# A DeepNorm layer with MoBA attention and 32 experts: routing chain in another order, V in the half slot of x transposed, two activation tiles and one Y buffer in a half slot

## The chip, the cores and the metric

The kernel runs on one core of a Trainium2 chip. Five engines work side by side, each through its own queue in program order: TensorE (PE in the rows; its weight loads are PEld), VectorE (DVE), ScalarE (ACT), GpSimd (POOL) and SyncE (SP), whose queue issues the DMA transfers. The metric is the device time of one launch in microseconds, and the number reported is the median of the runs.

## What is computed

One layer over 256 tokens of width 1024, in fp32. With the configuration cut to what is used:

```python
# attention: 8 heads of 128; 256 tokens are one block, so it is plain causal attention
# with a relative position bias
h = layer_norm(ALPHA * x + attention(x) @ w_out)
# mixture of experts: 32 experts, each token goes to its 4 best
logits = h @ w_router + b_router
top_logit, top_e = lax.top_k(logits, 4);  gate = softmax(top_logit)
# per expert, over the tokens that chose it
g, u = split(h @ w_gu[e] + b_gu[e])          # 1024 -> 2 x 1024
g = minimum(g, 7);  u = clip(u, -7, 7)
act = g * sigmoid(1.702 * g) * (u + 1)       # the swiglu
y = act @ w_down[e] + b_down[e]
out = layer_norm(ALPHA * h + sum over the 4 of gate * y)
```

The expert weights are 32 x 12 MB; together with the attention weights some 424 MB are read once.

## The kernel before, in words

**Weights.** `W_SLOTS` = 13 slots of 2 MB in SBUF, [128, 4096] fp32 each, hold everything large. `todo` lists all weight pieces in the order of use: six of `w_in`, two of `w_out`, then for every expert four of gate/up ("gu") and two of down ("dn"). Each time a slot comes free (`drop`, `done`) `prefetch` issues the next transfers on SP's queue (line 139), as many as there are free slots. The instruction that issues a load into a used slot waits until the matmuls that read the old contents have run; that wait stands in SP's queue, in order. Some slots hold no weights: `xhl` (the split of x), `BT_xT` (two halves: BT, later x and h; xT, later the accumulator `acc`), `QT_KTt` (two halves: QT, later the experts' biases; KTt, later the transposed rows `rT` and then `first`), `V`, and from the first expert on `acts_Ys`. That one holds three activation tiles g7, sg, u7, the transposed activation `aT`, and two buffers `Ys` for the outputs of a pair of experts.

**Order.** The program is scheduled by hand: every engine runs its instructions in the order in which the code issues them. There are eight PSUM banks with fixed names: `o0`, `o1`, `tp0`, `tp1`, `tp2`, `hg`, `hu`, `yp`. `o_tile()` hands out o0 and o1 in turn, `tp_tile()` tp0, tp1, tp2. A matmul into a bank waits until its last reader is done.

**Routing chain.** After the last piece of the attention's output projection (`out_part(3, ...)`, L431 to L434), for each of two token halves t: `residual` on VectorE (L440, with a piece of the statistics at L441, L191), the mean and the root (`Stats.root`, `finish`), the transposes of the rows (`rows_T`, L449) with a copy by ScalarE, the logits (L492, 16 matmul records of 32 columns), the four best (`top_experts`, VectorE, L499 to L504), the positions of the tokens in their experts' lists (`positions`, a matmul with a triangular matrix, L510), read by VectorE (`read_positions`, L514), one-hot matrices (L520), and the gather of the first pair's rows as matmuls with them (`first_gather`, L531). The two gather banks are zeroed ahead of that by an fp32 matmul of 512 columns each whose operands give zero (`open_gather`, L525). `stage1_bias` (L549) opens the banks hg and hu with the expert's bias, over 32 rows. Then stage 1 of expert 0 begins (L644).

**Experts.** Two experts make a pair, with 64 places for tokens each. For every expert the code issues, in this order: stage 1 (`stage1`, gate/up, L644, 64 matmul records per bank pair and weight piece); the `swiglu` on VectorE and ScalarE (L651, L652 on ScalarE, L653, L654, L655); half of the scatter of the pair before it (`pair_scatter`, L700, one token half t = s: a matmul into o0 and one into o1, each read by an add of VectorE into `acc`, L695); in odd experts from 3 on the gather of the next pair in two halves, the first ahead of the activation's transposes and the second behind them (L630; ScalarE reads the first half at L543, VectorE the second at L541); the transposes of the activation (`act_T`, L661) with a copy by ScalarE (L662); and stage 2 (`stage2`, down, L672). A matmul of fp32 with 512 columns is two records in the trace. Experts 17 and 19 also take in the residual (`add_residual`, each one half of the columns; L721 and L722 are its two steps on VectorE per token half, with a scratch value `tmp` in `first`), and expert 21 makes the list of experts with more than 64 tokens (`overflow_list`). Behind the last expert `more_blocks` loops over that list, and the last layer norm follows.

The lines that set the order around the change:

```python
            act = swiglu(hgu)
            Y = Ys[:, p % 2]
            if GT is not None:
                pair_scatter(GT, Y_old, s, p == 1)
```

## Time and profile before

| what | value |
|---|---|
| median of 3 runs | 1064.25 us (1064.24 to 1067.23) |
| the profiled execution | 1066.63 us |
| its span in the trace | 1064.8 us |
| TensorE matmul busy | 1017.2 us (96% of the span), 5008 records |
| VectorE busy | 261.5 us (25%) |
| ScalarE busy | 177.1 us (17%) |
| GpSimd busy | 7.4 us (1%) |
| moved by DMA | 425.33 MB, mean 399 GB/s; 426 to 429 GB/s in nearly every fortieth of the span from 160 us to 1010 us |

The profile's times are microseconds from the start of the span. A share of busy time is an average over stages with different limits, so the views by stretch and the waits are read beside it. "<-" in a row stands between an instruction's output and its inputs; in brackets behind a row is how long its engine had been idle before it, and whose end let it start.

### The profile page before, as it was taken

What the parts mean: (1) busy time and instruction counts of PE and PEld (TensorE: products, weight loads), DVE (VectorE), ACT (ScalarE), POOL (GpSimd) and SP (SyncE); (2) the same over time, 40 slices, a digit from 0 to 9 for tenths busy, and PEclk for the clock granted to TensorE, in tenths of its full rate; (3) what the DMA queues carried; (4) which work ended last, traced back from release to release, by engine and by line L of the source; (5) the groups of instructions that cost most, each with busy time, mean ns of one, the idle gap of its engine ahead of it and who ended that gap; (6) DMA issues with size and microseconds to landing.
All of it is one profiled execution on the core that took longest, in us unless ns stands there. A gap on an engine that the chain in (4) does not pass through costs nothing. (4 is left out here: it accounts for less than half of the span.)

```text
span 1064.8 us, 11698 instructions
## 1 busy us (share of the span) xinstructions
PE 1017.2 (96%) x5008; PEld 453.3 (43%) x5008; DVE 261.5 (25%) x554; ACT 177.1 (17%) x343; POOL 7.4 (1%) x8
## 2 busy tenths in 40 slices
PE   9999999999999999999999999999999999999994
PEld 8988743343433334343434343343434343434431
DVE  5576421121121111121212141211212121212114
ACT  5455121010100101010101010010101010101112
POOL 0000100000000000000000000000000000000001
PEclk9999799999999999999999999999999999999996
DMA  8987769999999999999999999999999999999971
GB/s 302 421 367 260 305 267 429 428 428 427 428 427 428 428 426 428 426 429 427 427 429 427 428 428 427 428 427 428 427 428 428 426 428 427 428 429 426 427 334 41
DMA packets 33110, 425.33 MB, mean 399 GB/s; under 512 B 3640, under 2 KB 4960, under 8 KB 7424
## 3 DMA queue, kind: packets, MB, share of 16 engines
q1 hardware_dynamic: 32784, 423.51, 94.4%
q10 hardware_dynamic: 272, 1.05, 0.3%
q8 instruction: 41, 0.67, 0.3%
q14 instruction: 13, 0.11, 0.0%
HBM read 423.48 MB, written 1.06 MB: 399 GB/s over the span
## 5 line engine op out<-in xcount | busy, mean ns | idle before, releaser
L644 PE MATMUL hg<-w,xg 128*64 128x512 f32 x960 | 248.2, 595 | 0.0
L644 PE MATMUL hu<-w,xg 128*64 128x512 f32 x960 | 246.6, 592 | 0.0
L672 PE MATMUL yp<-w,acts_Ys 128*64 128x512 f32 x1008 | 228.1, 598 | 11.2 <-ACT acts_Ys L662 11.2
L651 DVE TENSOR_SCALAR acts_Ys<-hg 128x512 f32<-128x512 f32 x32 | 22.1, 692 | 662.1 <-PE hg L644 653.6
L672 PEld LDWEIGHTS yp<-w,acts_Ys 128*64 128x64 f32 x1008 | 70.9, 137 | 146.1 <-issue 128.9
L644 PEld LDWEIGHTS hg<-w,xg 128*64 128x64 f32 x960 | 66.2, 137 | 144.3 <-issue 144.3
L644 PEld LDWEIGHTS hu<-w,xg 128*64 128x64 f32 x960 | 68.9, 137 | 137.2 <-issue 137.2
L652 ACT ACTIVATE acts_Ys<-acts_Ys 128x512 f32<-128x512 f32 x32 | 20.1, 630 | 459.5 <-DVE acts_Ys L651 459.5
L676 ACT COPY acts_Ys<-yp 64x512 f32<-64x512 f32 x63 | 36.5, 580 | 244.0 <-PE yp L672 236.9
L630 PE MATMUL tp<-OH,BT_xT 128*128 128x128 f32 x480 | 60.1, 279 | 9.7 <-ACT xg L543 9.7
L630 PEld LDWEIGHTS tp<-OH,BT_xT 128*128 128x128 f32 x480 | 56.7, 192 | 20.6 <-ACT xg L543 13.0
L700 PE MATMUL o<-acts_Ys,QT_KTt 128*128 128x512 f32 x120 | 59.5, 618 | 0.0
L166 DVE TENSOR_TENSOR whl<-w,whl 128x1024 fp32r<-128x1024 f32 (+1 forms) x36 | 38.2, 1103 | 23.5 <-ACT whl L177 23.5
L695 DVE TENSOR_TENSOR BT_xT<-o,BT_xT 128x512 f32<-128x512 f32 x60 | 38.6, 682 | 0.4
L700 PEld LDWEIGHTS o<-acts_Ys,QT_KTt 128*128 128x128 f32 x120 | 20.3, 189 | 38.7 <-issue 26.5
L177 ACT CAST whl<-w 128x1024 fp32r<-128x1024 f32 (+1 forms) x36 | 32.7, 955 | 15.3 <-DMA w<-in_w_in 6.3
L549 PE MATMUL hg<-QT_KTt,c 32*64 32x512 f32 x128 | 34.8, 620 | 0.0
L541 DVE TENSOR_SCALAR xg<-tp,c 128x128 f32<-128x128 f32 x60 | 20.5, 403 | 55.0 <-PE tp L630 55.0
L549 PE MATMUL hu<-QT_KTt,c 32*64 32x512 f32 x128 | 32.7, 587 | 0.0
L543 ACT ACTIVATE xg<-tp,c 128x128 f32<-128x128 f32 x60 | 22.6, 456 | 49.3 <-PE tp L630 49.3
L661 PE MATMUL tp<-c,acts_Ys 128*128 128x128 f32 x128 | 19.7, 277 | 6.7 <-DVE acts_Ys L655 6.7
L662 ACT COPY acts_Ys<-tp 128x512 f32<-128x512 f32 x32 | 18.9, 590 | 40.1 <-PE tp L661 40.1
(245 smaller groups left out, 723.1 us busy)
## 6 DMA issues: line engine op xcount, KB each, us to landing
w<-in_w_gu SPq DMA_DIRECT2D x128, 2048.0 KB, 28.7
w<-in_w_dn SPq DMA_DIRECT2D x63, 2048.0 KB, 27.5
w<-in_w_in SPq DMA_DIRECT2D x3, 2048.0 KB, 16.2
w<-in_w_in SPq DMA_DIRECT2D x4, 1024.0 KB, 11.1
w<-in_w_out SPq DMA_DIRECT2D x2, 2048.0 KB, 25.4
w<-in_w_dn SPq DMA_DIRECT2D x4, 512.0 KB, 30.0
w<-in_w_in SPq DMA_DIRECT2D x4, 256.0 KB, 5.0
w<-in_w_in SPq DMA_DIRECT2D x2, 512.0 KB, 7.9
```

The lines of the kernel that those rows point to most:

```text
L166: nc.vector.tensor_tensor(lo[:, s], w[:, s], hi[:, s].bitcast(F32), op=OP.subtract)
L177: nc.scalar.copy(o, i)
L541: nc.vector.tensor_scalar(o, i, g, b, op0=OP.mult, op1=OP.add)
L543: nc.scalar.activation(o, i, AF.Identity, scale=g, bias=b)
L549: nc.tensor.matmul(hgu[i][s * 64:(s + 1) * 64], onehot_e, bgu[:, 2 * i + s, :], start=True, stop=False)
L630: nc.tensor.matmul(ps[:, k * 128:(k + 1) * 128], h[:, t, kk * 128:(kk + 1) * 128], OH[:, t].rearrange("p s c -> p (s c)"), start=t == 0, s ...
L644: nc.tensor.matmul(hgu[i][s * 64:(s + 1) * 64], xg(k), w[:, kk, q * 512:(q + 1) * 512], start=False, stop=k == KT - 1)
L651: nc.vector.tensor_scalar(g7, hgu[0], LIMIT, None, op0=OP.min)
L672: nc.tensor.matmul(y_ps[s], aT[:, kk % 4, kk // 4, :], w[:, k, HALVES[s ^ swap]], start=kk == 0, stop=kk == KT - 1)
L676: copy(Y[s * 64:(s + 1) * 64, s ^ swap, :], y_ps[s])
L695: nc.vector.tensor_tensor(d, po, d, op=OP.add)
L700: nc.tensor.matmul(po, GT[:, cb, t, :], Y[:, cb, :], start=True, stop=True)
```

## The change

1. **V.** `V`, `first` and the biases take other halves: V lies where x transposed and later `acc` lie, `first` (the one-hots and gathered rows of the first pair) there too. The slot `V` is gone, with the `drop()` that gave it back.
2. **Activations.** Two activation tiles g7 and sg instead of three, with `aT` in g7's place, and one `Y` buffer instead of two, all in the half KTt. The clipped up half is written back to its PSUM bank (hu). The slot `acts_Ys` and the reserve that kept it free are gone. GT, the transposed gates, has a tile of its own, and `more_blocks` a slot `spare`.
3. **Scatter.** Both token halves of the pair's scatter follow stage 1 of the even expert, since Y is written again at its end; the odd expert has none.
4. **Residual.** `tmp` in `add_residual` lies in the banks o0 and o1.
5. **Routing chain.** The residuals are split from the statistics (`count`); logits of the first half are interleaved; the second half's experts are picked ahead of reading the first half's positions; the first expert's bias moves up to right behind the first positions; the gather banks are zeroed by bf16 matmuls with a tile of zeros; `filler(2)` puts two such matmuls ahead of the second half's gather; `rows_T` opens a bank per piece, with o0 for the third.
6. **Constants.** The constant tile shrinks from 641 to 452 columns, and `overflow_list` uses `ones`.

The core of the diff:

```diff
-    (BT, xT), (QT, KTt), (V, _) = (halves(slot(n)) for n in ("BT_xT", "QT_KTt", "V"))
-    x, acc, V = (t.rearrange("p (t d) -> p t d", t=2) for t in (BT, xT, V))
-    biases, first = QT, KTt
+    (BT, xT), (QT, KTt) = (halves(slot(n)) for n in ("BT_xT", "QT_KTt"))
+    x, acc = (t.rearrange("p (t d) -> p t d", t=2) for t in (BT, xT))
+    V, first, biases = acc, xT, QT
...
+    g7, sg = KTt[:, :512], KTt[:, 512:1024]
+    aT = g7.rearrange("p (j s c) -> p j s c", j=4, s=2)
+    Y = KTt[:, 1024:].rearrange("p (b c) -> p b c", b=2)
...
+    zeros = hp.tile([128, 512], BF, name="zeros")
...
         for ps in first_ps:
-            nc.tensor.matmul(ps, tri[:32, 0:1].to_broadcast([32, 128]), c[:32, :512], start=True, stop=False)
+            nc.tensor.matmul(ps, zeros[:, :128], zeros, start=True, stop=False)
+
+    def filler(n):
+
+        ps = bank("o0")
+        for i in range(n):
+            nc.tensor.matmul(ps, zeros[:, :128], zeros, start=i == 0, stop=i == n - 1)
...
+    logits(0, range(6, KT))
+    rows_T(1, 2, act_copy)
+    for i in range(3):
+        count(1, i)
+    logits(1)
     stats[1].root()
...
-    logits(1, range(6))
+    top_experts(0)
     stats[1].finish()
-    top_experts(0)
-    logits(1, range(6, KT))
     pp = positions(0)
+    hgu = stage1_bias(ident[:NE, 0:1].to_broadcast([NE, CAP]))
+    top_experts(1)
     read_positions(0, pp)
-    top_experts(1)
...
     pair_onehots(0, OH, slice(1, 2))
-    hgu = stage1_bias(ident[:NE, 0:1].to_broadcast([NE, CAP]))
+    filler(2)
     first_gather(1)
...
-        g7, sg, u7 = act3
+        u7 = hgu[1]
...
-        nc.vector.tensor_scalar(u7, hgu[1], LIMIT, -LIMIT, op0=OP.min, op1=OP.max)
+        nc.vector.tensor_scalar(u7, u7, LIMIT, -LIMIT, op0=OP.min, op1=OP.max)
...
-        tmp = first[:, :512]
         ps = tp_tile()
         spread(ps, 0, i)
         for t in range(2):
+            tmp = o_tile()
             nc.vector.scalar_tensor_tensor(tmp, h[:, t, cs], ALPHA, ps, op0=OP.mult, op1=OP.mult)
...
             act = swiglu(hgu)
-            Y = Ys[:, p % 2]
-            if GT is not None:
-                pair_scatter(GT, Y_old, s, p == 1)
+            if GT is not None and not s:
+                for t in range(2):
+                    pair_scatter(GT, Y, t, p == 1)
```

What it moves on the engines is shown at three places. A name ending in a number is one tile or one opening of a bank, "waits" names the engines whose semaphore the instruction waits for, and xN counts equal instructions in a row (two matmul records of the trace are one fp32 matmul here).

TensorE, the routing chain from the end of the logits to stage 1 of expert 0. tp0 and tp1 are the gather banks, M the chosen experts, hg and hu the banks of stage 1. Before:

```order
L492 MATMUL o1_1087<-oh_wg_83,QT_KTt_80 128x32 x8
L510 MATMUL tp2_1195<-M_954,c_68 128x32
L525 MATMUL tp0_1208<-c_68 128x512
L525 MATMUL tp1_1209<-c_68 128x512
L510 MATMUL tp2_1212<-M_954,ones_73 128x32
L510 MATMUL tp2_1212<-M_954,c_68 128x32
L531 MATMUL tp0_1208<-QT_KTt_80,BT_xT_79 128x128 x4
L531 MATMUL tp1_1209<-QT_KTt_80,BT_xT_79 128x128 x4
L549 MATMUL hg_1225<-QT_KTt_80,c_68 64x512 x2
L549 MATMUL hu_1226<-QT_KTt_80,c_68 64x512 x2
L531 MATMUL tp0_1208<-QT_KTt_80,BT_xT_79 128x128 x4
L531 MATMUL tp1_1209<-QT_KTt_80,BT_xT_79 128x128 x4
```

The same stretch of TensorE's queue now, from right behind the first half's positions (L508) to the filler; the second half's gather follows:

```order
L553 MATMUL hg_1199<-QT_KTt_80,c_68 64x512 x2
L553 MATMUL hu_1200<-QT_KTt_80,c_68 64x512 x2
L523 LDWEIGHTS zeros_84
L523 MATMUL tp0_1216<-zeros_84 128x512
L523 LDWEIGHTS zeros_84
L523 MATMUL tp1_1217<-zeros_84 128x512
L508 MATMUL tp2_1220<-M_955,ones_73 128x32
L508 MATMUL tp2_1220<-M_955,c_68 128x32
L535 MATMUL tp0_1216<-BT_xT_79 128x128 x4
L535 MATMUL tp1_1217<-BT_xT_79 128x128 x4
L529 LDWEIGHTS zeros_84
L529 MATMUL o0_1233<-zeros_84 128x512
```

The bias (hg, hu) has moved from between the two gathers to behind the first positions, the zeroing reads the tile of zeros, and zero matmuls into o0 stand ahead of the second half's gather.

TensorE, even expert 26, from the end of stage 1 (L644, now L651) to stage 2 (L672, now L679). o0 and o1 take the scatter, tp2 the activation's transposes. Before:

```order
L644 MATMUL hu_4069<-w_3938,xg_4001 64x512 x2
L700 MATMUL o0_4119<-acts_Ys_1311,QT_KTt_80 128x512 [waits Activation_49]
L700 MATMUL o1_4122<-acts_Ys_1311,QT_KTt_80 128x512
L661 MATMUL tp2_4125<-c_68,acts_Ys_1311 128x128 [waits DVE_49,PE_49]
L661 MATMUL tp2_4125<-c_68,acts_Ys_1311 128x128 x3
L672 MATMUL yp_4131<-w_3956,acts_Ys_1311 64x512 [waits DMAHW3_49,Activation_49]
```

The same stretch now:

```order
L651 MATMUL hu_4090<-w_3954,xg_4021 64x512 x2
L707 MATMUL o0_4140<-QT_KTt_80,GT_4046 128x512 [waits Activation_49]
L707 MATMUL o1_4143<-QT_KTt_80,GT_4046 128x512
L707 MATMUL o0_4146<-QT_KTt_80,GT_4046 128x512 [waits DVE_49]
L707 MATMUL o1_4149<-QT_KTt_80,GT_4046 128x512 [waits DVE_49]
L668 MATMUL tp2_4152<-c_68,QT_KTt_80 128x128 [waits PE_49]
L668 MATMUL tp2_4152<-c_68,QT_KTt_80 128x128 x3
L679 MATMUL yp_4158<-w_3964,QT_KTt_80 64x512 [waits DMAHW3_49,Activation_49]
```

Two scatter matmuls have become four, and the third and fourth wait for VectorE.

VectorE, the same expert, before:

```order
L651 TENSOR_SCALAR acts_Ys_1311<-hg_4068 128x512 [waits DVE_49,PE_49]
L653 TENSOR_SCALAR acts_Ys_1311<-hu_4069 128x512 [waits PE_49]
L654 TENSOR_TENSOR acts_Ys_1311<-acts_Ys_1311 128x512 [waits Activation_49]
L655 SCALAR_TENSOR_TENSOR acts_Ys_1311<-acts_Ys_1311 128x512 [waits DVE_49]
L695 TENSOR_TENSOR BT_xT_79<-o0_4119,BT_xT_79 128x512 [waits PE_49]
L695 TENSOR_TENSOR BT_xT_79<-o1_4122,BT_xT_79 128x512 [waits PE_49]
```

And now:

```order
L658 TENSOR_SCALAR QT_KTt_80<-hg_4089 128x512 [waits PE_49,Activation_49]
L660 TENSOR_SCALAR hu_4090<-hu_4090 128x512 [waits PE_49]
L661 TENSOR_TENSOR QT_KTt_80<-QT_KTt_80 128x512 [waits Activation_49]
L662 SCALAR_TENSOR_TENSOR QT_KTt_80<-hu_4090,QT_KTt_80 128x512 [waits DVE_49]
L702 TENSOR_TENSOR BT_xT_79<-o0_4140,BT_xT_79 128x512 [waits PE_49]
L702 TENSOR_TENSOR BT_xT_79<-o1_4143,BT_xT_79 128x512 [waits PE_49]
L702 TENSOR_TENSOR BT_xT_79<-o0_4146,BT_xT_79 128x512 [waits PE_49]
L702 TENSOR_TENSOR BT_xT_79<-o1_4149,BT_xT_79 128x512 [waits PE_49]
```

The swiglu's four steps stand ahead of the adds in both, and there are four adds instead of two; the clipped up half is written to hu.

## Rows read from the trace of the kernel before

**Rows 1.** Busy time by stretch: stretch and length, PE, PEld, DVE, ACT, POOL, PEclk, DMA, GB/s.

```profile
500.00:600.00 100.00, 97.53 (x468) 37.68 (x464) 18.44 (x39) 11.52 (x23) 0.00 (x0) 1.00 1.01 428
1036.20:1042.80 6.60, 6.60 (x32) 2.01 (x28) 0.00 (x0) 0.00 (x0) 0.00 (x0) 1.00 0.00 0
```

**Rows 2.** Waits of SP's queue: line, what it waited for, us in all, times, longest.

```profile
SPq L139 <- PE hu L644: 396.2, 112, 23.2
SPq L139 <- DMA w<-in_w_gu: 66.6, 23, 4.5
```

**Rows 3.** Waits of TensorE, same columns.

```profile
PE tp L661 <- DVE acts_Ys L655: 6.7, 17, 2.1
```

**Rows 4.** Busy time by stretch, routing chain.

```profile
116.60:120.00 3.40, 3.24 (x16) 3.24 (x16) 1.27 (x7) 0.48 (x2) 0.20 (x1) 0.50 0.98 414
126.80:130.30 3.50, 3.50 (x17) 2.65 (x17) 0.00 (x0) 0.00 (x0) 0.00 (x0) 0.50 0.01 2
```

**Rows 5.** TensorE in order of time, routing chain: start, us, instructions, [idle before <-releaser].

```profile
102.01 0.62 PE L434 MATMUL o<-whl,xhl 128*128 128x512 f32 x2
...
120.52 0.61 PE L510 MATMUL tp<-M,c 128*128 128x32 f32 x2
121.06 3.78 PE L525 MATMUL tp<-c 32*128 32x512 f32 x4
...
125.64 3.76 PE L531 MATMUL tp<-QT_KTt,BT_xT 128*128 128x128 f32 x16
...
131.65 2.05 PE L531 MATMUL tp<-QT_KTt,BT_xT 128*128 128x128 f32 x16
```

**Rows 6.** VectorE in order of time, routing chain.

```profile
113.11 0.69 DVE L191 BATCH_NORM_STATS2 st_a<-BT_xT 128x6 f32<-128x512 f32 x1
...
121.17 0.19 DVE L514 SCALAR_TENSOR_TENSOR posm<-M,tp 128x32 f32<-128x32 f32 x1 [3.12 <-PE tp L510]
...
122.36 0.19 DVE L504 TENSOR_TENSOR M<-lg,rest 128x32 f32<-128x32 f32 x1
```

**Rows 7.** TensorE in order of time, expert 26.

```profile
889.91 1.98 PE L700 MATMUL o<-acts_Ys,QT_KTt 128*128 128x512 f32 x4
892.20 0.63 PE L661 MATMUL tp<-c,acts_Ys 128*128 128x128 f32 x4 [0.30 <-DVE acts_Ys L655]
893.55 7.09 PE L672 MATMUL yp<-w,acts_Ys 128*64 128x512 f32 x32 [0.73 <-ACT acts_Ys L662]
```

**Rows 8.** VectorE in order of time, expert 26.

```profile
890.03 0.69 DVE L653 TENSOR_SCALAR acts_Ys<-hu 128x512 f32<-128x512 f32 x1 [0.17 <-PE hu L644]
...
891.36 0.69 DVE L655 SCALAR_TENSOR_TENSOR acts_Ys<-acts_Ys 128x512 f32<-128x512 f32 x1
891.97 1.28 DVE L695 TENSOR_TENSOR BT_xT<-o,BT_xT 128x512 f32<-128x512 f32 x2
```

**Rows 9.** TensorE in order of time, expert 27.

```profile
916.32 1.98 PE L700 MATMUL o<-acts_Ys,QT_KTt 128*128 128x512 f32 x4
918.14 1.95 PE L630 MATMUL tp<-OH,BT_xT 128*128 128x128 f32 x16
...
921.68 2.05 PE L630 MATMUL tp<-OH,BT_xT 128*128 128x128 f32 x16 [0.72 <-ACT xg L543]
```

**Rows 10.** VectorE in order of time, expert 19.

```profile
690.62 0.69 DVE L721 SCALAR_TENSOR_TENSOR QT_KTt<-BT_xT,tp 128x512 f32<-128x512 f32 x1
```

**Rows 11.** TensorE in order of time, expert 19.

```profile
685.94 1.98 PE L700 MATMUL o<-acts_Ys,QT_KTt 128*128 128x512 f32 x4
...
691.54 2.05 PE L630 MATMUL tp<-OH,BT_xT 128*128 128x128 f32 x16
```

**Rows 12.** TensorE in order of time, expert 1.

```profile
177.41 0.66 PE L661 MATMUL tp<-c,acts_Ys 128*128 128x128 f32 x4 [2.12 <-DVE acts_Ys L655]
178.80 8.40 PE L672 MATMUL yp<-w,acts_Ys 128*64 128x512 f32 x32
```

**Rows 13.** TensorE in order of time, expert 31.

```profile
1034.39 0.63 PE L661 MATMUL tp<-c,acts_Ys 128*128 128x128 f32 x4 [0.29 <-DVE acts_Ys L655]
```

More of the change, by code (lines that the diff above doesn't have):

```diff
@@ L36 @@
 GU, DN = 4, 2
-C_ID, C_IOTA, C_E32, C_TRI, C_EV, C_CV, C_PM, C_LN = 0, 128, 256, 288, 416, 512, 608, 609
+C_ID, C_IOTA, C_E32, C_TRI, C_CV, C_PM, C_LN = 0, 128, 256, 288, 416, 419, 420
 C_W = C_LN + 4 * KT
@@ L47, in shape_consts @@
     c[:, C_TRI:C_TRI + 128] = np.triu(np.ones((128, 128)), 1)
-    c[:, C_EV:C_EV + 96] = np.tile(np.arange(32), 3)
-    c[:, C_CV:C_CV + 96] = np.repeat(CAP * np.arange(1, 4), 32)
+    c[:, C_CV:C_CV + 3] = CAP * np.arange(1, 4)
     c[:, C_PM] = np.arange(128) % 32
@@ L251, in tile_decoder_layer @@
     nc.vector.memset(rrow[:, 0:127], NEG)
+    nc.vector.memset(zeros, 0.0)
     rd = dr.tile([H, 383], F32, name="rd")
@@ L440, in residual, with count @@
         nc.vector.scalar_tensor_tensor(rc, rc, ALPHA, ps, op0=OP.mult, op1=OP.add)
-        stats[t].add(cb, rc)
+    def count(t, cb):
+        stats[t].add(cb, x[:, t, PIECES[t][cb]])
     def rows_T(t, cb, copy):
         s = PIECES[t][cb]
-        k0, k1 = s.start // 128, s.stop // 128
-        ps = T_ps[t, k0 // 4]
-        for kk in range(k0, k1):
-            nc.tensor.transpose(ps[:, kk % 4 * 128:(kk % 4 + 1) * 128], x[:, t, kk * 128:(kk + 1) * 128], ident)
-        copy(rT[:, k0:k1, t * 128:(t + 1) * 128],
-             ps[:, k0 % 4 * 128:((k1 - 1) % 4 + 1) * 128].rearrange("p (k c) -> p k c", c=128))
-    T_ps = {}
-    def open_T(t):
-        for q, n in enumerate(ROWS_T):
-            T_ps[t, q] = bank(n)
+        k0, n = s.start // 128, (s.stop - s.start) // 128
+        ps = bank((ROWS_T + ("o0",))[cb])
+        for i in range(n):
+            nc.tensor.transpose(ps[:, i * 128:(i + 1) * 128], x[:, t, (k0 + i) * 128:(k0 + i + 1) * 128], ident)
+        copy(rT[:, k0:k0 + n, t * 128:(t + 1) * 128], ps[:, :n * 128].rearrange("p (k c) -> p k c", c=128))
     sums = small("sums", 2 * NE)
@@ L524, in open_gather @@
         for ps in first_ps:
-            nc.tensor.matmul(ps, tri[:32, 0:1].to_broadcast([32, 128]), c[:32, :512], start=True, stop=False)
+            nc.tensor.matmul(ps, zeros[:, :128], zeros, start=True, stop=False)
+    def filler(n):
+        ps = bank("o0")
+        for i in range(n):
+            nc.tensor.matmul(ps, zeros[:, :128], zeros, start=i == 0, stop=i == n - 1)
     def first_gather(t):
@@ L685, in pair_slots_T @@
         if GT is None:
-            GT = first[:, 1536:].rearrange("p (b t c) -> p b t c", b=2, t=2)
+            GT = mp.tile([128, 2, 2, 2 * CAP], F32, name="GT")
         nc.scalar.copy(GT, ps.rearrange("p (b t c) -> p b t c", b=2, t=2))
@@ L738, in overflow_list @@
         fl = small("fl", 96)
-        one96 = small("one96", 96)
-        nc.vector.memset(one96, 1.0)
         nc.vector.tensor_tensor(fl.rearrange("p (k e) -> p k e", k=3),
                                 cnt[:, None, :].to_broadcast([128, 3, NE]),
-                                c[:, C_CV:C_CV + 96].rearrange("p (k e) -> p k e", k=3), op=OP.is_gt)
-        nc.vector.tensor_tensor_scan(om, one96, fl, 0.0, op0=OP.mult, op1=OP.add)
+                                c[:, C_CV:C_CV + 3][:, :, None].to_broadcast([128, 3, NE]), op=OP.is_gt)
+        nc.vector.tensor_tensor_scan(om, ones[:, :96], fl, 0.0, op0=OP.mult, op1=OP.add)
         nc.vector.tensor_copy(n_i, om[:, 95:96])
@@ L757, in more_blocks @@
         bufs = itertools.cycle([slot("lw") for _ in range(2)])
-        spare = first
+        spare = slot("spare")
         Y2 = spare[:, :1024].rearrange("p (b c) -> p b c", b=2)
@@ L842, in tile_decoder_layer @@
                 pair_onehots(2 * p + 2, OH, slice(0, 2))
-            if e == 0:
-                acts, Ys = halves(slot("acts_Ys"))
-                act3 = [acts[:, i * 512:(i + 1) * 512] for i in range(3)]
-                aT = acts[:, 1536:].rearrange("p (j s c) -> p j s c", j=4, s=2)
-                Ys = Ys.rearrange("p (i b c) -> p i b c", i=2, b=2)
-                reserve[0] = 0
             act = swiglu(hgu)
-            Y = Ys[:, p % 2]
-            if GT is not None:
-                pair_scatter(GT, Y_old, s, p == 1)
+            if GT is not None and not s:
+                for t in range(2):
+                    pair_scatter(GT, Y, t, p == 1)
             if e in (17, 19):
```

41 lines of the change are left out of this document (19 added, 22 removed).

## The prediction

> **What bounds the kernel now.** I read the views in this order: who waits for whom on the queue that issues the weight loads, what TensorE waits for, the busy time by stretch, and then one expert after the other in order of time. The DMA engines look like the bound: from 500 to 600 us they are busy all the time at 428 GB/s, while TensorE shows 97.53 us of work in 100 [rows 1]. The waits say the opposite. The issuing queue spends 396.2 us in 112 waits until a gate/up matmul gives a weight slot back, and only 66.6 us in waits for an earlier load [rows 2]. TensorE's list holds no wait for a load at all; the largest wait for a finished swiglu is 6.7 us in all [rows 3]. At the end no load runs from 1036.2 us on, while TensorE works on to 1042.8 [rows 1]. So TensorE's own queue, in program order, is the path from the first gather to the last down projection. A microsecond that it idles between two experts ends up in the time; weights that come earlier don't.
>
> All sums start from the profiled execution, 1066.63 us (span 1064.8 and 1.8 around it). The median of the timed runs, 1064.25, lies 2.4 us lower; I take that off at the end.
>
> **The change part by part.** *Routing chain.* [...] Four parts of the change act here. The zeroing of the two gather banks was 3.78 us of fp32 matmuls [rows 5]; two one-pass matmuls of that width take 0.62 us [rows 5]. VectorE stood for 3.12 us waiting for the first positions before it picked the second half's experts [rows 6]; now it picks first and reads the positions afterwards. The experts' bias matmuls move into the gap while VectorE picks. Two zero matmuls (0.62 us) are added ahead of the second gather. At full clock: the wait of 3.12 us ended at 121.17, and the pick behind it at 122.36 + 0.19 = 122.55 [rows 6], so without the wait it ends near 119.4; but two of the second half's three statistics, 0.69 us for the large one [rows 6] and about half of that for the next, now come behind its last residual, and this residual behind logits: I put 1.3 us on it, 120.7. Then the positions (0.3, half of a group that took 0.61 [rows 5]), gather 2.05, zeros 0.62, gather 2.05: the first expert's stage 1 starts near 125.7 instead of 133.7 (131.65 + 2.05), a gain of 8.0. If the clock falls all the same, the two gathers and the bias are stretched to what they took before, some 4 us: a gain of 4.0. The bias matmuls use 32 rows of the array, and ahead of them lie the small logits and positions, which is the mix after which the clock fell before; so I take a part of it, 5.3. GpSimd's normalisation of the first half starts later too, and I take it to end ahead of the gather, which alone needs it.
>
> *Even experts, 2 to 30.* Both token halves of the pair's scatter now follow stage 1 of the even expert: four matmuls over two banks, o0, o1, o0, o1. The third needs o0 read out, and VectorE's queue has the swiglu ahead of that read. From expert 26: the scatter starts at 889.91 [rows 7], the swiglu's last step ends at 891.36 + 0.69 = 892.05, the two adds take 1.28 us from 891.97 [rows 8], so the first ends at 892.61. TensorE follows VectorE by 0.15 (892.05 to 892.20 [rows 7, 8]): third matmul at 892.76. Two matmuls take 1.9 (1.98 with the tail [rows 7]), so the transposes of the activation start near 894.6 instead of 892.20, and everything behind by as much: +2.4. The 0.30 us wait that stood there [rows 7] is in that difference. 15 experts: +36.0.
>
> *Odd experts, 3 to 29.* Their scatter is gone. The gather's first half starts at 916.32 instead of 918.14, ScalarE's read of it and the second half, which waits for that read, move along [rows 9]: -1.82. The swiglu doesn't stop this: it is ready 2.29 us after stage 1 (892.20 - 889.91), that is at 918.61, and two groups of transposes end by 919.5, before the second half's new start of 919.86. 12 plain experts: -21.8. So a pair gets 0.6 us longer, not shorter: the scatter's cover is taken from the odd expert, and the even one can't use it because its banks run out.
>
> *Experts 17 and 19* hold the residual as well. Its scratch value moves into the banks o0 and o1, so its two bias matmuls must wait for VectorE: the first for two instructions behind the swiglu, the second for four, at 0.69 us each [rows 10] and 0.72 with the hand-over from one to the next. Swiglu 2.1, four times 0.72, hand-over 0.15, matmul 0.95: the gather starts 6.0 us after stage 1 instead of 691.54 - 685.94 = 5.6 [rows 11], and 19 costs +0.3; 17, which had a further matmul group on its path, gains about as much. Together 0. But TensorE now stands for 1.8 and 0.5 us there with only 32-row matmuls between.
>
> *Clock between experts.* Expert 1 shows what such a stop costs: 2.12 us of waiting for the swiglu without cover [rows 12], and the down projection then took 8.40 us instead of 7.09 [rows 7, 12]: 1.3 us at the lower clock. 17 and 19 now look like that: +2.6. Expert 31 loses its scatter; its transposes can't start earlier, since the swiglu held them by 0.29 already [rows 13], but it waits 2.29 us with nothing to do: three chances in four of 1.3, +1.0.
>
> *Slots.* V in the free half of the transposed x, and activations in the half that held the transposed rows, free one slot each: the stream runs one 2 MB load ahead. Nothing waits for it; the cover is that TensorE is the later of the two. Worth 0. If TensorE got more than about 6 us faster (1036.2 against 1042.8 [rows 1]), the slot would be needed.
>
> *Swiglu in the bank.* The clipped half stays in PSUM, so VectorE writes there, which no row shows; the nearest is the same step writing SBUF, 0.69, and the step that has SBUF alone takes 0.69 as well [rows 8]. I take no change, and 0.1 us either way in 15 even experts, 1.5 us, for the range. [...]
>
> *At no cost:* the memset of the zeros (VectorE waits for x then), smaller constants (a load that nobody waits for), the own tile of the transposed gates, the shorter overflow list.
>
> Sum: 1066.63 - 5.3 + 36.0 - 21.8 + 0 + 2.6 + 1.0 = 1079.1; less 2.4 for the median, 1076.7. I say 1077.
>
> **The rivals.** *A: the scatter doesn't wait, so faster or even.* If the third matmul got its bank without standing behind the swiglu (adds reached early enough), four matmuls would run through: the even expert's transposes start 3.8 us after stage 1, not 2.29, +1.5 less 0.1; 15 times 1.4 is 21, and the odd experts give 21.8 back. Only routing and clock remain: 1076.7 - 15 = 1062. Against it: VectorE works in program order, the swiglu's last step ends at 892.05 [rows 8], and o0 is full at about 890.9. It decides if the adds end before 891.8.
>
> *B: the stream is the bound, so faster.* The DMA engines run without a gap at 428 GB/s [rows 1]. If TensorE's matmuls hid waits for weights, the stream's end would set the time, TensorE's new stops would be free, and a slot more would start the stream earlier by one load, 2 MB at 428 GB/s or 4.9 us, beside the routing's 5.3: 1064.25 - 10.2 = 1054. [...] Against it stand the 112 waits for TensorE's release and no wait of TensorE for a load [rows 2, 3].
>
> *C: the routing chain doesn't keep its clock.* It gives 4.0, not 5.3: 1078. For it: small and 32-row matmuls remain. Same sign.
>
> **How the numbers follow.** About 0.3%, 3.2 us, is what a measurement tells from no change. Forecast with C, slower: 0.85. A: 0.08, half of it under 1061. B: 0.04. Something between, stops partly hidden: 0.03, within. So faster 0.08, same 0.06, slower 0.86. Low end: no clock fall in 17, 19, 31 (-3.6) and the whole routing gain (-2.7), 1070. High end: routing 4.0 (+1.3), PSUM 1.5, hand-overs 0.1 longer in 15 experts (1.5), the median's 2.4 not found again: 1083. A and B lie outside, with 0.12.
>
> **What would show it.** In an even expert four scatter matmuls with about 1 us of idle time ahead of the third, released by VectorE's add, and 6.0 us from stage 1 to the down projection instead of 3.6; in an odd one 5.5 instead of 7.3; in 17 and 19 a stretch at 0.50. Stage 1 of expert 0 near 128.4, and no load that TensorE waits for. I am wrong if the even expert shows no such gap, if TensorE waits for weights, or if stage 1 starts much before 125 us.

## The result, and the profile after

The changed kernel takes 1072.43 us (median; 1071.03 to 1073.85) against 1064.24 us (1062.68 to 1067.23) for the kernel before: 1.0075 of its time, with an interval of 1.0056 to 1.0094. It is slower, by 8.2 us. The profiled execution took 1072.28 us with a span of 1070.5. Single executions of the kernel before lie apart with the clock (in a later set 1062.77 us at a mean granted clock of 0.989 and 1072.49 at 0.980), so some of them reach the changed kernel's time; the account by place below rests on the two traces and not on the medians.

The even experts show what was forecast. TensorE in order of time, even expert 26 of the changed kernel (start, us, instructions, [idle before <-releaser]); it answers to [rows 7]:

```profile
896.73 1.98 PE L707 MATMUL o<-QT_KTt,GT 128*128 128x512 f32 x4
899.52 1.98 PE L707 MATMUL o<-QT_KTt,GT 128*128 128x512 f32 x4 [0.81 <-DVE BT_xT L702]
901.34 0.60 PE L668 MATMUL tp<-c,QT_KTt 128*128 128x128 f32 x4
902.62 7.09 PE L679 MATMUL yp<-w,QT_KTt 128*64 128x512 f32 x32 [0.68 <-ACT QT_KTt L669]
```

VectorE beside it, as in [rows 8]:

```profile
898.18 0.69 DVE L662 SCALAR_TENSOR_TENSOR QT_KTt<-hu,QT_KTt 128x512 f32<-128x512 f32 x1
898.78 1.28 DVE L702 TENSOR_TENSOR BT_xT<-o,BT_xT 128x512 f32<-128x512 f32 x2
```

The third scatter matmul stands for 0.81 us and is let go by VectorE's first add, which stands behind the last step of the swiglu and begins at 898.78. From the start of the scatter to the down projection it takes 902.62 - 896.73 = 5.89 us; before, it was 893.55 - 889.91 = 3.64 [rows 7]. The odd expert behind it has lost its scatter, and the gather comes at once; this answers to [rows 9]:

```profile
925.38 2.05 PE L637 MATMUL tp<-OH,BT_xT 128*128 128x128 f32 x16
927.57 0.66 PE L668 MATMUL tp<-c,QT_KTt 128*128 128x128 f32 x4
928.06 0.60 PE L690 MATMUL tp<-c,Gd 128*128 128x128 f32 x4
929.02 2.05 PE L637 MATMUL tp<-OH,BT_xT 128*128 128x128 f32 x16 [0.36 <-ACT xg L547]
931.01 7.09 PE L679 MATMUL yp<-w,QT_KTt 128*64 128x512 f32 x32
```

931.01 - 925.38 = 5.63 us. In the kernel before, the down projection of expert 27 starts here:

```profile
923.66 7.09 PE L672 MATMUL yp<-w,acts_Ys 128*64 128x512 f32 x32
```

So it took 923.66 - 916.32 = 7.34 us [rows 9]. The twelve plain odd experts got 1.72 us shorter on average, and so each pair got 2.25 - 1.72 = 0.53 us longer. In TensorE's list of waits (line, what it waited for, us in all, times, longest) the new one is at the top, and there is no load of weights among them:

```profile
PE o L707 <- DVE BT_xT L702: 12.0, 14, 1.2
PE yp L679 <- ACT QT_KTt L669: 10.6, 17, 0.7
```

TensorE in the routing chain, from right behind the first half's positions to stage 1, as in [rows 5]:

```profile
118.98 1.75 PE L553 MATMUL hg<-QT_KTt,c 32*64 32x512 f32 x4
120.51 1.92 PE L553 MATMUL hu<-QT_KTt,c 32*64 32x512 f32 x4
122.36 1.03 PE L523 MATMUL tp<-zeros 128*128 128x512 bf16 x2
...
123.90 3.06 PE L535 MATMUL tp<-BT_xT 128*128 128x128 f32 x16
126.80 0.59 PE L529 MATMUL o<-zeros 128*128 128x512 bf16 x2
127.23 1.95 PE L535 MATMUL tp<-BT_xT 128*128 128x128 f32 x16
129.11 1.08 PE L651 MATMUL hg<-w,BT_xT 128*64 128x512 f32 x4
```

Stage 1 of expert 0 starts at 129.11 instead of 133.63. Counted from the first transposes of the rows (110.78 before, 111.41 after), the chain went from 22.85 to 17.70 us. The granted clock still fell in it, but for about 6.8 us (0.51 from 119.2 to 126.1) and not 13.7 (0.50 from 116.6 to 130.3). Busy time by stretch (stretch, length, PE, PEld, DVE, ACT, POOL, PEclk, DMA, GB/s); it answers to [rows 4]:

```profile
120.00:126.00 6.00, 6.00 (x22) 3.51 (x19) 1.38 (x9) 1.52 (x2) 0.00 (x0) 0.50 0.99 419
126.20:129.10 2.90, 2.90 (x25) 2.63 (x24) 0.00 (x0) 0.78 (x3) 0.00 (x0) 1.00 0.37 153
```

One thing was not in the forecast at all: the end of the span got shorter. TensorE's last group, the scatter behind the loop over further blocks, before:

```profile
1046.99 6.11 PE L884 MATMUL o<-acts_Ys,QT_KTt 128*128 128x512 f32 x8 [4.16 <-issue]
```

and after:

```profile
1055.01 3.90 PE L882 MATMUL o<-QT_KTt,GT 128*128 128x512 f32 x8 [1.70 <-DVEq L770]
```

From the start of the last down projection to the end of the span it is 1064.8 - 1035.75 = 29.05 us before and 1070.5 - 1046.23 = 24.27 after.

The whole difference of the two spans, 5.7 us, by place (all from the starts of stage 1 and of the down projection of each expert):

| place | forecast, us | measured, us |
|---|---|---|
| up to stage 1 of expert 0 | -5.3 | -4.5 |
| 15 even experts | +36.0 | +34.5 |
| 12 odd experts | -21.8 | -20.6 |
| experts 17 and 19, clock included | +2.6 | -0.5 and +1.5 |
| experts 1 and 31 | +1.0 | +0.1 |
| behind the start of the last down projection | 0 | -4.8 |
| sum | +12.5 | +5.7 |

### The profile page after: what moved, and what is told of

Same layout as the page of the kernel before. It is cut to its first block, busy times and chain, and to the rows that moved or that the text cites. A ratio compares the mean times of both kernels' runs of the same rounds, so it can differ in the third digit from the quotient of the medians.

```text
span 1070.5 us, 11658 instructions
## 1 busy us (share of the span) xinstructions
PE 1016.2 (95%) x5008; PEld 452.2 (42%) x5008; DVE 264.1 (25%) x554; ACT 176.8 (17%) x343; POOL 7.4 (1%) x8
## 3 DMA queue, kind: packets, MB, share of 16 engines
HBM read 423.38 MB, written 1.06 MB: 396 GB/s over the span
## 5 line engine op out<-in xcount | busy, mean ns | idle before, releaser
L651 PE MATMUL hg<-w,xg 128*64 128x512 f32 x960 | 248.2, 595 | 0.0
L651 PE MATMUL hu<-w,xg 128*64 128x512 f32 x960 | 246.6, 592 | 0.0
L679 PE MATMUL yp<-w,QT_KTt 128*64 128x512 f32 x1008 | 228.3, 599 | 10.6 <-ACT QT_KTt L669 10.6
L658 DVE TENSOR_SCALAR QT_KTt<-hg 128x512 f32<-128x512 f32 x32 | 22.1, 692 | 665.8 <-PE hg L651 665.8
L679 PEld LDWEIGHTS yp<-w,QT_KTt 128*64 128x64 f32 x1008 | 70.9, 138 | 145.5 <-issue 129.1
L651 PEld LDWEIGHTS hg<-w,xg 128*64 128x64 f32 x960 | 66.2, 137 | 144.4 <-issue 143.6
L651 PEld LDWEIGHTS hu<-w,xg 128*64 128x64 f32 x960 | 68.8, 137 | 137.2 <-issue 137.2
L659 ACT ACTIVATE QT_KTt<-QT_KTt 128x512 f32<-128x512 f32 x32 | 20.1, 629 | 459.8 <-DVE QT_KTt L658 459.8
L683 ACT COPY QT_KTt<-yp 64x512 f32<-64x512 f32 x63 | 36.5, 579 | 244.4 <-PE yp L679 237.4
L707 PE MATMUL o<-QT_KTt,GT 128*128 128x512 f32 x120 | 59.5, 618 | 12.8 <-DVE BT_xT L702 12.0
L637 PE MATMUL tp<-OH,BT_xT 128*128 128x128 f32 x480 | 62.5, 285 | 5.7 <-ACT xg L547 5.7
L707 PEld LDWEIGHTS o<-QT_KTt,GT 128*128 128x128 f32 x120 | 20.3, 188 | 51.8 <-DVE BT_xT L702 27.8
L669 ACT COPY QT_KTt<-tp 128x512 f32<-128x512 f32 x32 | 18.9, 590 | 73.6 <-PE tp L668 73.6
L668 PE MATMUL tp<-c,QT_KTt 128*128 128x128 f32 x128 | 20.3, 282 | 5.9 <-DVE QT_KTt L662 4.3
```

The lines of the kernel that those rows point to most:

```text
L637: nc.tensor.matmul(ps[:, k * 128:(k + 1) * 128], h[:, t, kk * 128:(kk + 1) * 128], OH[:, t].rearrange("p s c -> p (s c)"), start=t == 0, s ...
L651: nc.tensor.matmul(hgu[i][s * 64:(s + 1) * 64], xg(k), w[:, kk, q * 512:(q + 1) * 512], start=False, stop=k == KT - 1)
L658: nc.vector.tensor_scalar(g7, hgu[0], LIMIT, None, op0=OP.min)
L679: nc.tensor.matmul(y_ps[s], aT[:, kk % 4, kk // 4, :], w[:, k, HALVES[s ^ swap]], start=kk == 0, stop=kk == KT - 1)
L683: copy(Y[s * 64:(s + 1) * 64, s ^ swap, :], y_ps[s])
L707: nc.tensor.matmul(po, GT[:, cb, t, :], Y[:, cb, :], start=True, stop=True)
```

## The experiments

The theory to test: the third scatter matmul waits for a bank whose read stands behind the swiglu in VectorE's queue. The rival that the trace of the changed kernel leaves open: an even expert is longer simply because it holds twice the scatter's matmuls. Further runs take the routing chain, experts 17 and 19, and the end apart. "Plain" experts are the even ones from 2 and the odd ones from 3 on, without 17, 19 and 31.

### The second half behind the transposes

```diff
-            if GT is not None and not s:
-                for t in range(2):
-                    pair_scatter(GT, Y, t, p == 1)
+            if GT is not None and not s:
+                pair_scatter(GT, Y, 0, p == 1)
...
             act_T(act)
+            if GT is not None and not s:
+                pair_scatter(GT, Y, 1, p == 1)
```

> The changed kernel with the scatter of the second token half moved behind the transposes of the activation in the even experts; nothing else. Theory (the third scatter matmul waits for VectorE, whose queue has the swiglu ahead of the read of the bank): behind the transposes the bank is long read, and the two matmuls stand where TensorE waited for ScalarE's copy (0.68 us), so the stretch from stage 1 to the down projection of an even expert falls from 5.88 to about 4.8 us, odd ones stay at 5.63; 15 x 1.05 = 15.7 us less than the changed kernel, 1072.4 to 1057. Rival (an even expert is longer because it now holds twice the scatter's matmuls, wherever they stand): 5.7 to 5.9 us, 1070 to 1072.

Measured: 1056.5 us (1056.18 to 1057.66), 0.9912 of the kernel before (0.988 to 0.9943). Expert 26 of this kernel on TensorE:

```profile
880.42 1.98 PE L707 MATMUL o<-QT_KTt,GT 128*128 128x512 f32 x4
882.71 0.63 PE L668 MATMUL tp<-c,QT_KTt 128*128 128x128 f32 x4 [0.30 <-DVE QT_KTt L662]
883.21 1.98 PE L707 MATMUL o<-QT_KTt,GT 128*128 128x512 f32 x4
885.13 1.08 PE L679 MATMUL yp<-w,QT_KTt 128*64 128x512 f32 x4
```

The same eight records take 885.13 - 880.42 = 4.71 us instead of 5.89. The two matmuls that had waited now stand where TensorE stood anyway for ScalarE's copy (0.68 us in the changed kernel). The number of matmuls is the same, so the rival falls as the whole explanation: of the 2.25 us that expert 26 had lost, 1.18 come back by the place alone. The other 1.07 (4.71 against 3.64) stay with the two additional matmuls, and what the odd expert gave up more than pays for them: a pair now takes 4.71 + 5.63 = 10.34 us, 0.64 less than the 10.98 of the kernel before. Of the 15.9 us between the spans of the two changed kernels the even experts give 17.0 and the routing chain's start of stage 1 another 1.9; the end takes 3.2 back.

### The second half in other banks

```diff
-            po = o_tile()
+            po = tp_tile() if t else o_tile()
             nc.tensor.matmul(po, GT[:, cb, t, :], Y[:, cb, :], start=True, stop=True)
```

> The changed kernel with the second token half of the scatter in two of the three tp banks instead of o0 and o1 again; the order is as it was. Theory (bank wait): the four matmuls run through in 3.8 us with no wait for VectorE, the transposes follow at once, and the stretch of an even expert falls from 5.88 to about 5.15 us; 15 x 0.75 = 11 us, 1072.4 to 1061. Rival (work, not the banks): no wait to remove, 5.9 us, 1072.

Measured: 1057.01 us (1054.12 to 1059.48), 0.9914 of the kernel before (0.9884 to 0.9944). Expert 26:

```profile
882.84 1.98 PE L707 MATMUL o<-QT_KTt,GT 128*128 128x512 f32 x4
884.66 1.88 PE L707 MATMUL tp<-QT_KTt,GT 128*128 128x512 f32 x4
886.37 0.60 PE L668 MATMUL tp<-c,QT_KTt 128*128 128x128 f32 x4
887.65 1.94 PE L679 MATMUL yp<-w,QT_KTt 128*64 128x512 f32 x8 [0.68 <-ACT QT_KTt L669]
```

With the order untouched and only the banks changed, the four matmuls run through: 887.65 - 882.84 = 4.81 us, 1.08 less than in the changed kernel. That is more than the 0.75 that was expected, mostly because the four took 886.37 - 882.84 = 3.53 us and not 3.8. This is rival A of the prediction, made true by two more banks: it was a question of the banks, and with nothing else moved the wait for them is the 1.08 us.

### Two Y buffers, scatter as before

```diff
-    Y = KTt[:, 1024:].rearrange("p (b c) -> p b c", b=2)
+    Ys = slot("Ys")[:, :2048].rearrange("p (i b c) -> p i b c", i=2, b=2)
...
+        Y_old = Ys[:, (p + 1) % 2]
...
-            if GT is not None and not s:
-                for t in range(2):
-                    pair_scatter(GT, Y, t, p == 1)
+            Y = Ys[:, p % 2]
+            if GT is not None:
+                pair_scatter(GT, Y_old, s, p == 1)
```

> The changed kernel with two Y buffers again, in a slot of their own, and the scatter as before, one token half per expert; routing chain, activation tiles and the rest as changed, one weight slot fewer than the changed kernel. Theory (the grouping of the scatter alone makes the expert loop longer, the slots are worth nothing): even experts 3.64, odd 7.35 us again, so 34.4 - 20.6 = 13.8 us less, 1072.4 to 1058.6, and no load that TensorE waits for. Rival (the free slots carry part of the time, or the swiglu in the bank does): even experts stay above 3.8 us, or TensorE waits for loads; 1061 or more.

Measured: 1064.28 us (1061.85 to 1066.98), 0.9978 of the kernel before (0.9957 to 0.9999). The plain experts are at 3.58 us (even) and 7.34 (odd) again; expert 27:

```profile
915.63 1.98 PE L707 MATMUL o<-Ys,GT 128*128 128x512 f32 x4
922.97 1.51 PE L679 MATMUL yp<-w,QT_KTt 128*64 128x512 f32 x6
```

TensorE waits for no load of weights with one slot fewer, so the grouping over two banks alone made the plain experts longer. But the time is 5.7 us above what was expected, and by the time alone the rival (1061 or more) would have been right; the places decide against it. Two of them cost 9.2 us: 17 and 19 went to 14.46 and 15.40 us (11.52 and 12.77 in the changed kernel), and the end to 27.9 us (24.3), with a stop of 3.66 us ahead of the last scatter; the routing chain gave 2.4 back. In 17 the scatter of the odd expert now shares o0 and o1 with the residual's scratch value, and the gather behind the wait of 0.77 us is stretched:

```profile
623.02 2.36 PE L736 MATMUL o<-QT_KTt 32*128 32x512 f32 x4 [0.77 <-DVE BT_xT L729]
625.31 3.31 PE L637 MATMUL tp<-OH,BT_xT 128*128 128x128 f32 x16
```

The gather takes 3.31 us there instead of 2.05 (in expert 19 of the changed kernel 3.30, where the granted clock was 0.50). The expectation had left 17, 19 and the end out.

### A wait less in the odd experts as well

On top of the first experiment, the second half of the gather goes into a bank o:

```diff
         def quarter(q):
-            ps = tp_tile()
+            ps = o_tile() if q else tp_tile()
```

> The kernel with the second half of the scatter behind the transposes, and in addition the second half of the odd experts' gather in a bank o instead of the third tp bank, so that it doesn't wait for ScalarE's read of the first half (0.36 us ahead of it in expert 27 of the changed kernel). Theory (TensorE's queue is the bound, so each wait taken out of it comes off the time): the stretch of an odd expert falls from 5.63 to about 5.3 us, 13 experts with such a gather and 17 and 19 beside: 14 x 0.36 = 5 us, 1056.5 to 1051.5. Rival (by now the stream of weights holds TensorE, or ScalarE's copy of the activation does): the wait moves to the down projection, 1056.

Measured: 1056.2 us (1053.86 to 1057.84), 0.9902 of the kernel before (0.9876 to 0.9927): no gain over the first experiment. The odd experts did get shorter, 5.00 us instead of 5.63; expert 27:

```profile
904.80 2.05 PE L637 MATMUL tp<-OH,BT_xT 128*128 128x128 f32 x16
...
907.92 1.95 PE L637 MATMUL o<-OH,BT_xT 128*128 128x128 f32 x16
909.80 1.51 PE L679 MATMUL yp<-w,QT_KTt 128*64 128x512 f32 x6
```

What they gave came back as something that no earlier kernel shows, waits of TensorE for a load of weights; the first of seven:

```profile
871.66 1.08 PE L651 MATMUL hg<-w,xg 128*64 128x512 f32 x4 [0.95 <-DMA w<-in_w_gu]
```

Stage 1 of experts 26 to 30, from its start to the next group, grew from 13.88 us by 1.17, 2.10, 1.80, 1.88 and 1.74, 8.7 us in all, which is more than the 12 x 0.63 = 7.6 that the plain odd experts gave. In the queue that issues the loads, the waits have turned over. The changed kernel:

```profile
SPq L138 <- PE hu L651: 440.1, 121, 16.7
```

and this one:

```profile
SPq L138 <- DMA w<-in_w_gu: 294.8, 72, 5.9
SPq L138 <- PE hu L651: 217.6, 64, 16.6
```

The other places nearly cancel (the routing chain and expert 19 1.5 us longer each; expert 1 shorter by 1.6, the end by 1.4, 17 by 1.0). So the stream of weights is the bound from about 1056 us down: the rival of the expectation holds, and rival B of the prediction, wrong for this change, is right 16 us further on.

### The routing chain, part by part

Four kernels, each with one part of the new chain undone and each executed once, in the order below 1075.4, 1076.11, 1071.83 and 1073.29 us; the measure is the stretch from the first transposes of the rows to stage 1 of expert 0. It is 22.85 us before and 17.70 in the changed kernel; the kernels of the first and the third experiment, which have the same chain, took 16.04 us, with the bias matmuls at 1.07 and 1.02 us each instead of 1.75 and 1.92, and the first gather at 3.26 and 3.48 instead of 3.06. By an estimate from these lengths the clock was low in them for some 3.4 us instead of 6.8. How long the clock is low belongs to each figure; for the four kernels it is given as such an estimate, with the groups that are stretched.

The zeroing in fp32 again:

```diff
-            nc.tensor.matmul(ps, zeros[:, :128], zeros, start=True, stop=False)
+            nc.tensor.matmul(ps, tri[:32, 0:1].to_broadcast([32, 128]), bgu[:, 0, :], start=True, stop=False)
```

> The changed kernel with the gather banks zeroed by fp32 matmuls over 32 rows as before (operands with the product zero), nothing else. From the first transposes of the rows (111.41) to stage 1 of expert 0 (129.11) the changed kernel took 17.7 us. Theory: the zeroing took 1.03 us there and took 3.78 us before, both at the lower clock: 1.3 us more at the full clock, 2.7 at the lower one, 19.0 to 20.4 us. Rival (the zeroing lies beside VectorE's pick and costs nothing): 17.7.

133.45 - 112.57 = 20.88 us, 3.2 more and 0.5 above the range that was expected, with the first gather at 3.76 us and the second at 2.42 (3.06 and 1.95 in the changed kernel): the clock was low for an estimated 10 us. The zeroing is in the path with its full length, 2.75 us more than the 1.03 of the changed kernel, where the granted clock was 0.50 (122.36 to 123.40); 3.78 us is also what it took at 0.50 in the kernel before [rows 5]:

```profile
122.11 3.78 PE L523 MATMUL tp<-QT_KTt,c 32*128 32x512 f32 x4
```

Without the zero matmuls ahead of the second gather:

```diff
-    filler(2)
```

> The changed kernel without the two zero matmuls ahead of the second half's gather. Theory (they only add their time, 0.43 us from their start to the gather's): 17.3 us from the first transposes of the rows to stage 1 instead of 17.7. Rival (they bring the clock back): the clock rises later, the second gather takes over 3 us instead of 1.95: 18.4 us or more.

128.78 - 111.53 = 17.25 us, 0.45 less, with the bias matmuls at 1.40 and 1.92 us: the clock was low for an estimated 6.8 us, as in the changed kernel. They cost their time and bring nothing back here: in the changed kernel the granted clock was 1.00 from 126.2 on, ahead of them (126.80), and here the two gathers take 5.18 us together, less than two of the 3.76 that one takes at 0.50 [rows 5], so it came up without them.

VectorE reads the positions first again:

```diff
+    read_positions(0, pp)
     top_experts(1)
-    read_positions(0, pp)
```

> The changed kernel with VectorE reading the first half's positions ahead of picking the second half's experts, as before. The prediction gave this order 3.12 us. Theory of the prediction: VectorE stands for the positions again and 2 to 3 us are lost, 20 us or more from the first transposes of the rows to stage 1. Rival (the wait was that long because the positions stood behind 3.46 us of logits in TensorE's queue, and those now stand ahead): the positions are there 0.8 us after the pick, four short steps of the statistics lie between, and 0.2 us are lost, 17.9 us.

128.62 - 110.92 = 17.70 us, with the bias matmuls at 1.86 and 1.92 us and the first gather at 2.96, so with the clock low for an estimated 6.8 us: nothing lost. VectorE no longer waits there:

```profile
118.65 0.21 DVE L203 TENSOR_SCALAR rs_a<-rs_a 128x1 f32<-128x1 f32 x1
118.78 0.18 DVE L512 SCALAR_TENSOR_TENSOR posm<-M,tp 128x32 f32<-128x32 f32 x1
```

The 3.12 us of [rows 6] were a wait for TensorE, whose queue had 3.46 us of logits ahead of the positions:

```profile
117.24 3.46 PE L492 MATMUL o<-oh_wg,QT_KTt 128*128 128x32 f32 x16
```

In the changed kernel TensorE is through with the logits 0.34 us before the first positions can start (118.64), and the order on VectorE is worth nothing.

The bias matmuls back behind the first gather:

```diff
-    hgu = stage1_bias(ident[:NE, 0:1].to_broadcast([NE, CAP]))
     top_experts(1)
...
+    hgu = stage1_bias(ident[:NE, 0:1].to_broadcast([NE, CAP]))
     filler(2)
```

> The changed kernel with the first expert's bias matmuls back behind the first half's gather (ahead of the zero matmuls), as before. Theory (in the changed order they fill the time in which VectorE picks the second half's experts, 1.2 to 1.9 us of it): 1.2 to 2 us more from the first transposes of the rows to stage 1 than the 17.7 of the changed kernel, or the 16.0 where the clock stays low only half as long. Rival (they hide nothing, since TensorE is the path there anyway): the same 16 to 17.7 us.

128.10 - 110.61 = 17.49 us, with the bias matmuls at 1.25 and 1.02 us and the first gather at 3.45, so with the clock low for an estimated 3.4 us, and 1.45 more than the 16.04 of the kernels with as short a fall. TensorE then stands 1.22 us for VectorE:

```profile
119.90 0.41 PE L508 MATMUL tp<-M,ones 128*128 128x32 f32 x2 [1.22 <-DVE posm L512]
```

### The scratch value of the residual

```diff
+    resid = slot("resid")[:, :512]
...
         for t in range(2):
-            tmp = o_tile()
+            tmp = resid
```

> The changed kernel with the scratch value of the residual (experts 17 and 19) in a slot of its own in SBUF instead of the banks o0 and o1; one weight slot fewer. Theory (the bias matmuls wait for VectorE only because the scratch value holds their banks: 1.00 us in 17, 1.46 and 0.21 us in 19): 17 goes from 11.52 to about 10.5, 19 from 12.77 to 10 or 11, the latter if the clock falls there all the same. Rival (they wait for the swiglu's part of VectorE's queue in any case): within 0.3 us of 11.5 and 12.8.

17 fell to 10.08 and 19 to 9.52 us, each below what was expected and together 4.7 less than in the changed kernel, and the one execution took 1068.13 us. In 19 the bias matmuls follow the spread at once, and the gather behind them takes 2.05 us instead of the 3.30 of the changed kernel, so by that length the clock stayed up:

```profile
687.42 2.05 PE L715 MATMUL tp<-c 128*128 128x128 f32 x16
689.40 1.98 PE L737 MATMUL o<-QT_KTt 32*128 32x512 f32 x4
691.31 2.05 PE L638 MATMUL tp<-OH,BT_xT 128*128 128x128 f32 x16
```

### The end

The kernel before once more, with nothing edited.

> The kernel before, once more. In the profile of before TensorE stood 4.16 us ahead of the last scatter, behind the loop over further blocks, and 1.70 us in the changed one; the last scatter then took 6.11 and 3.90 us. Theory (where the code lies decides how long its loading takes after the loop is skipped): the same program shows about 4.2 and 6.1 us again. Rival (chance of each execution): some other value, as 1.7 and 3.9.

The same program shows the same stop in a second execution (1067.32 us): 4.35 us, and 6.01 us for the group.

```profile
1047.81 6.01 PE L884 MATMUL o<-acts_Ys,QT_KTt 128*128 128x512 f32 x8 [4.35 <-issue]
```

Then the kernel before with its program moved:

```diff
         nc.tensor.matmul(warm[:, :128], ones, ones, start=i == 0, stop=i == 8)
+    for _ in range(24):
+        nc.tensor.matmul(warm[:, :4], ones, ones[:, :4], start=True, stop=True)
```

> The kernel before with 24 more small matmuls (4 columns, result unused) at the very start, which move everything behind them in TensorE's program; they delay the start by some us, and only the end is read. Theory (how TensorE's program lies in the pieces in which it is loaded decides the 4.2 us it stands ahead of the last scatter): another value than 4.2 us, 1.7 if the piece is already there, or a stop at another place of the last matmuls. Rival (a wait for data or another engine): 4.2 us again.

```profile
1049.58 3.90 PE L886 MATMUL o<-acts_Ys,QT_KTt 128*128 128x512 f32 x8 [1.77 <-DVEq L767]
```

Same data, same slots, same work at the end, and the stop is 1.77 us and the group 3.90, as in the changed kernel. The start came some 5 us later (stage 1 of expert 0 at 138.62) and the end gave 4.7 back; the execution took 1066.85 us.

The same lines added to the changed kernel:

> The changed kernel with the same 24 small matmuls at the start. Theory (place of the program): the 1.70 us ahead of the last scatter can become some 4 us or a stop can appear among its eight matmul records, as in the kernel with the scatter's half moved (1.65 us behind the first); or nothing changes if the pieces still end well. Rival (the changed kernel's end is shorter for its data or slots): 1.70 us and 3.90 us again.

Measured: 1.82 us and 3.90, so its end stays short there, which fits the theory and its rival alike; the execution took 1080.04 us, with stage 1 of expert 0 at 135.95. The first experiment's kernel, whose program differs from the changed one in the order of the matmuls, stops in the middle of the group:

```profile
1035.92 0.70 PE L883 MATMUL o<-QT_KTt,GT 128*128 128x512 f32 x1 [1.70 <-DVEq L770]
1038.26 4.97 PE L883 MATMUL o<-QT_KTt,GT 128*128 128x512 f32 x7 [1.65 <-issue]
```

So the end is no effect of the slots or the scatter: the kernel before has the short end once its program is moved, and two kernels built on the changed one have a longer one (the first experiment's, and the one with two Y buffers, where TensorE stood 3.66 us). What the 24 matmuls change at the end is where the program lies; that this is how they act is inferred.

## Why the prediction was right, point by point

**What bounds.** Right: TensorE's queue set the time, each stop between stage 1 and the down projection came out in the end, and no load of weights was waited for. (The list of the kernel before does hold one load: 0.2 us at 13 us, for a table at the start.) How near the other bound lay was put at about 6 us below the kernel before ("if TensorE got more than about 6 us faster"); the loads were first felt some 8 us below it, at 1056.

**Even experts.** Right, by place and releaser; +2.25 us each instead of +2.4, 34.5 instead of 36.0. Forecast and trace have the third matmul 2.85 and 2.79 us behind the first. Experts 10 and 30 lost 0.35 and 0.4 more than the others. The experiments with other banks and another place confirm the mechanism; they put 1.1 to 1.2 of the 2.25 us on the wait and the rest on the two additional matmuls (rival A had put 1.4 of 2.4 on those).

**Odd experts.** Right: -1.72 each instead of -1.82. The second half of the gather comes 3.64 us behind the first, where it was 3.54, since ScalarE's read of the first half still lets it go [rows 9].

**Experts 17 and 19.** The waits came where they were put, behind VectorE's steps with the scratch value, but shorter: 1.00 us in 17, 1.46 and 0.21 in 19, against 1.8 and 0.5. The prediction's own terms give 6.08 us up to 19's gather and not 6.0, so 0.5 more than before and not 0.3; measured are 695.54 - 689.64 = 5.90, 0.3 more. What was mis-sized is the clock: the forecast had it fall in both, at 1.3 us each; it fell in 19 alone (0.50 from 696.2 to 699.4 us, the gather at 3.30 us instead of 2.05). In 17 the gather took 3.78 us in the kernel without the zero matmuls and 3.31 in the one with two Y buffers, so there, by these lengths, the clock fell. And "together 0" for the rest hides a cost: without the scratch value in the banks both would have gained by the scatter that left them, as the run with the slot shows (10.08 and 9.52 against 11.99 and 11.24 before).

**Clock in expert 31.** Three chances in four for a fall were too many. TensorE stood 2.21 us for the swiglu, as in expert 1 (2.12), where the clock did fall (0.50); in 31 it did not (1.00). Of the ten traced kernels without a scatter in expert 31 three show the first matmuls of its down projection stretched, at 1.06 us instead of 0.59. The stretches of the two waits and what follows, expert 1 and expert 31:

```profile
174.20:177.00 2.80, 2.78 (x8) 0.93 (x10) 0.72 (x4) 0.46 (x1) 0.00 (x0) 0.50 1.05 445
1042.20:1046.20 4.00, 1.57 (x12) 0.86 (x8) 2.45 (x4) 1.24 (x3) 0.00 (x0) 1.00 0.00 0
```

**Routing chain.** The size was about right (-4.5; by its own stretch -5.15), and that is in part luck, because one of its reasons fails and the clock fell for half as long as before, which is neither of the two cases that it was weighed from. The second case, some 4 us more, stands on the one gather's 3.76 us at a granted clock of 0.50 and 2.05 at 1.00 [rows 4, 5]; the two of the changed kernel took 3.06 and 1.95. The pick ahead of the positions, put at 3.12 us, gives nothing. Undoing the zeroing costs 3.2 us, undoing the bias in the gap 1.45, and the zero matmuls ahead of the second gather take 0.45. These don't add up to the 5.15, since by the lengths of the groups the clock was low for a different time in some of these kernels; how much of the 5.15 is the shorter fall (6.8 us instead of 13.7) no run shows by itself. An estimate: the same chain took 16.04 us with the clock low for some 3.4 us (itself estimated from the lengths of the groups) and 17.70 with 6.8, so 3.4 us at the lower clock cost 1.66, and 6.8 us less of it may be some 3.3 of the 5.15.

**Slots, swiglu in the bank.** Both worth nothing, as forecast: a slot fewer left the plain experts as they were, and the step that writes PSUM (L660) takes 0.70 us against 0.69 [rows 8]. The last step, which now has a source in PSUM (L662), takes 0.69 us as before.

**The sum.** The point lay 4.6 us above the measured median. The largest miss is a term that wasn't there, the end's -4.8; the clock falls that did not come make another 2.5 (1.5 in 17 and 19, 1.0 in 31). Against that the 2.4 us taken off for the median were not found: the profiled execution of the changed kernel lies at its median. The loop's own sum is no luck: its two large terms came out within 1.5 us each. That the time lies in the range although the end was left out is helped by a range 13 us wide and by misses of opposite sign.

## What to carry to other kernels

Two rounds of the same banks in a row waited here for the reader's queue (0.81 us in expert 26, behind the swiglu's last step), not for the reader's speed: look at what stands ahead of the read on that engine, and put the second round behind other work or into other banks (here 16 us, from 1072.4 to 1056.5, which is below the kernel before). Grouping the scatter was not the loss in itself: over the same two banks it made a pair 0.53 us longer, without the bank wait 0.64 us shorter. Where work only covered a wait, taking it away gave nothing: expert 31 without its scatter got 0.05 us shorter. And when an engine's waits are gone, look at the next bound before removing more: here it was reached after 16 us, and a further 7.6 us of waits bought nothing.

## What the runs showed of the hardware that was not expected

- Behind a loop that isn't entered, TensorE stood 4.16 us (4.35 in a second execution) ahead of its next matmul, and 1.77 us after 24 unused matmuls had been put at the start of the same program. In the long stop instruction packets move on two queues (in the stretch from 1042.8 to 1047.0 us of the kernel before one of 0.02 MB and one of 0.01 MB); in the short stops of the changed kernel and of the shifted one it is the one of 0.02 MB alone. That the stop is the loading of that code is inferred from this and from the shift; no run shows that TensorE waited for these packets.
- The stop cost more than itself. The granted clock fell in it (0.76 in the stop, 0.50 behind it), and the eight matmul records behind it took 6.11 us instead of the 3.90 of the changed kernel, where it was 1.00. Busy time by stretch of the kernel before, in the stop and behind it:

```profile
1043.00:1047.00 4.00, 0.01 (x1) 0.01 (x1) 0.66 (x2) 1.73 (x2) 0.00 (x0) 0.76 0.02 6
1047.00:1051.80 4.80, 4.80 (x6) 2.03 (x7) 1.61 (x5) 0.01 (x1) 0.00 (x0) 0.50 0.02 3
```

- Behind the same wait of 2.1 to 2.2 us the granted clock was 0.50 in expert 1 and 1.00 in expert 31 of one execution (the changed kernel's), and expert 17 kept it in one kernel and lost it in another with the same code there (14.00 us, the gather 3.78, in the kernel without the zero matmuls; 11.52 and 2.05 in the changed one). A fall of the clock behind such a stop was worth 1.3 to 2.5 us: 8.40 and 8.58 us instead of 7.09 for the down projection of expert 1 in the kernel before and in the changed one, 6.11 instead of 3.90 at the end, 14.00 instead of 11.52 in 17. What decides between a fall and none, no run here shows.
